# High and low parts of x computed once, kept in DRAM, and loaded by five later stages

## The chip, the cores and the metric

The kernel runs on one core of one Trainium2 chip. The core has a matrix engine (TensorE, PE in the profile; its weight loads are PEld), a vector engine (DVE), a scalar engine (ACT), a general engine (POOL) and a sequencer that here issues all DMAs (SP). Each engine works through its own instructions in order and waits on semaphores for the others. Tiles lie in the on-chip memory (SBUF), matmul results in PSUM; DRAM is reached by DMA, and all DMAs of this kernel go through one queue, fed by SP, onto 16 DMA engines. The metric is device time in microseconds (us). Three runs of the kernel before took 1255.81, 1256.64 and 1258.46 us; the median is 1256.64 us.

## The reference, cut to what matters

One decoder layer over 2048 tokens of width 1024. What is computed:

```python
hdn = rmsnorm(x, norm_gain[i])
proj = jnp.einsum("bsd,de->bse", hdn, w_in[i])
q_a, k_a, v_a, g_a, q_b, k_b, v_b, g_b = jnp.split(proj, split_at, axis=-1)
# mixer A: 8 query heads, 2 key heads, causal window of 128 tokens, attention sinks
q_a = rope(rmsnorm(q_a...), pos); k_a = rope(rmsnorm(k_a...), pos)
o_a, _, _ = banded_attention(q_a, k_a, v_a, A_WINDOW - 1, sinks=sinks_a[i])
o_a = o_a * jax.nn.silu(g_a)
# mixer B: 8 heads, patterns (128,1), (512,4), (2048,16), merged by their denominators
q_b = rope(rmsnorm(q_b...), pos); k_b = rope(rmsnorm(k_b...), pos)
o_b = dilated_attention(q_b, k_b, v_b) * jax.nn.silu(g_b)
mixed = jnp.concatenate([o_a, o_b], axis=-1)
x = x + jnp.einsum("bse,ed->bsd", mixed, w_out[i])
```

All of it is float32. The part that matters here is the product `hdn @ w_in`: its left factor x is the same for all of its columns.

## The kernel before

**Stages.** The work is cut into eight stages (`STAGES`): B0 to B3 (two heads of mixer B each), A0 and A1 (four heads of mixer A each), and O0 and O1 (half of the output projection's columns each). A stage walks over the 2048 tokens in eight halves of 256 tokens (`hf` 0 to 7; two of them make one block `sb`). For each half it makes the q/k/v projection of two groups of 128 tokens (matmuls 384 wide, or 256 wide in O), then the gate projection (256 wide), and hands the result to attention work that is issued in between.

**Three matmuls for one product.** TensorE takes float32 in the rounded form `float32r`. To keep the precision, each factor is split into a high part (the value rounded to float32r) and a low part (the rest), and `mm3` (L241 to L244) adds three products, high*high, high*low and low*high. So a half of x (1 MB, eight chunks of 128 rows by 256 tokens) needs its high parts `xh` and low parts `xl` on the chip.

**Where x comes from.** `x_load` (L145 to L149) loads half of a half, 512 KB, from the input `xT` (or from `mx`, the gated attention output, in O) into a tile `xs`, of which there are two. `x_split` (L151 to L158) takes a quarter: ACT copies it into `xh`, rounding it (L155), and POOL or DVE subtracts (L157): POOL for the quarters 0 and 1, and for all quarters of the halves 6 and 7, DVE for the rest. Six pairs of `xh` and `xl` take turns (`XB`), four for the current half and two of the next. Each of the eight stages does this for each half anew; only the very first half goes another way (`first_half`, in eight pieces). The quarters 2 and 3 of the next half are split during the gate matmuls of the current one, because their tiles are those that these matmuls read last.

**What else a half does.** In B0, `squares` sums x*x for the norm, `rstd` makes the inverse root, `rb_make` spreads it over the partitions, and `rope_tables` makes the rotary tables. POOL's `klz` (L90) writes zeros once, at the start. In each half `norm_rope` takes the projection from PSUM, `norm_factors` (POOL, L182 and L437, `fac`) and `norm_split` (DVE, L447) normalise it, and `finish` transposes q and k on TensorE. A B stage stores q, k, v, gates and sums to DRAM (`qd`, `kd`, `ld`, `vd`, `gd`, `od`), and the next stage loads them by residue class (`units_D`: `cq`, `ck`, `cl`, `cv`); at the end of such a unit the softmax factors go to DRAM (`rD`) and come back spread over the partitions (`Rb`, one buffer, two rounds of two loads), and POOL multiplies with them (L899 to L906).

**Weights.** During the last half of a stage and the first of the next, the next stage's weights come in twelve tiles (eight `stg` of the projection, L118, and the gates', L131; three buffers) and are split by ACT and DVE (`split_w`).

**What sets the order.** The program is written in Python as one stream in which attention units are interleaved with projection chunks by estimated costs (`advance`, `pcost`). A scheduler then sets each engine's order of instructions by a timeline of its own; so DMAs from different places of the program stand mixed on SP's queue, and a changed instruction can move others.

Of the kernel before, what the change touches and what calls it, by code (L numbers as in the profile page):

```python
# [18 lines left out]
KC = DM // 128  # L19
EPS = 1e-6  # L20
WB = 9
XB = 6
QB = {"Q": 2, "qc": 2}
SB = 3
BIG = 1e30
# [3 lines left out]
def f32(ap):  # L29
    return ap.bitcast(F32)  # L30
# [3 lines left out]
def hybrid_layer(ctx, tc, xT, xn, x, wB, wA, wO, ng, gains, sinks, rot, masks, ident, out):  # L34
# [9 lines left out]
    def dram(shape, name, dt=F32):  # L44
        return tc.dram_tile(shape, dt, name=name)
# [44 lines left out]
                nc.gpsimd.tensor_scalar(zt, mk[z, 0:640], 0.0, None, op0=OP.mult)  # L90

    rs_row = [dram([256], f"rsr{hf}") for hf in range(8)]
    mx = [dram([128, KC, 256], f"mx{hf}") for hf in range(8)]

    def bcast_row(d, lo, n, parts=128):
# [44 lines left out]
    XG = {}  # L140

    XS = {}
    SQ = []

    def x_load(si, hf, g):  # L145
        src = mx[hf] if STAGES[si][0] == "O" else xT[hf]
        f = xp.tile([128, 4, 256], F32, name="xs")
        nc.sync.dma_start(f, src[:, 4 * g:4 * g + 4, :])
        XS[si, hf, g] = f  # L149

    def x_split(si, hf, g):  # L151
        f = XS[si, hf, g // 2][:, 2 * (g % 2):2 * (g % 2) + 2]
        h = xp.tile([128, 2, 256], F32R, name="xh", bufs=XB)
        l = xp.tile([128, 2, 256], F32R, name="xl", bufs=XB)
        nc.scalar.activation(h, f, AF.Copy)  # L155
        eng = nc.gpsimd if g < 2 or hf >= 6 else nc.vector
        eng.tensor_tensor(l, f, f32(h), op=OP.subtract)  # L157
        XG[si, hf, g] = (h, l)  # L158

    def first_half():  # L160
        for g in range(4):
            if g % 2 == 0:
                XS[0, 0, g // 2] = xp.tile([128, 4, 256], F32, name="xs")
            f = XS[0, 0, g // 2][:, 2 * (g % 2):2 * (g % 2) + 2]
            h = xp.tile([128, 2, 256], F32R, name="xh", bufs=XB)
            l = xp.tile([128, 2, 256], F32R, name="xl", bufs=XB)
            for c in range(2):
                nc.sync.dma_start(f[:, c], xT[0][:, 2 * g + c, :])
                W[0][2](2 * g + c, lambda: (nc.scalar.activation(h[:, c], f[:, c], AF.Copy),
                                            nc.vector.tensor_tensor(l[:, c], f[:, c], f32(h[:, c]), op=OP.subtract)))  # L170
            XG[0, 0, g] = (h, l)
        for g in range(2):
            squares(XS[0, 0, g], g)

# [71 lines left out]
    def proj(si, sb):  # L246
# [22 lines left out]
        for half in range(2):  # L269
            hf = 2 * sb + half  # L270
            nx = next_half(si, hf)
            xg = [XG.pop((si, hf, g)) for g in range(4)]
            TC, TS = TB.pop((si, hf))
            if nx:
                x_load(*nx, 0)
            t1s = []
            un = wk.tile([128, 2, nh], F32, name="un")
            for tt in range(2):
                i = 2 * half + tt
                T = 4 * sb + i  # L280
                pj = ps.tile([128, 384], F32, name="sc" if early and half else "pj", bufs=2)
                for c in range(KC):
                    xh, xl = xg[c // 2]
                    s = slice(tt * 128, tt * 128 + 128)
                    mm3(pj, (xh[:, c % 2, s], xl[:, c % 2, s]), wq[c], c, c == 0, c == KC - 1)
                    if last and half == 1 and tt == 1:
                        W[si + 1][2](c)
                    if nx and tt == 1 and c == 3:
                        x_split(*nx, 1)
                    yield 490  # L290
                if tt == 0 and nx:
                    x_load(*nx, 1)
# [18 lines left out]
                nc.vector.scalar_tensor_tensor(vt[:, :, 1, :], vs, rst[:, T:T + 1], f32(vt[:, :, 0, :]),  # L311
                                               op0=OP.mult, op1=OP.subtract)
# [203 lines left out]
    def proj_out(si, sb, wq, wg, last):  # L516
# [4 lines left out]
        for half in range(2):  # L521
            hf = 2 * sb + half
            nx = next_half(si, hf)
            xg = [XG.pop((si, hf, g)) for g in range(4)]
            if nx:
                x_load(*nx, 0)
                x_load(*nx, 1)
# [512 lines left out]
```

## Time and profile before

The profiled execution took 1261.51 us; its span, from the first instruction to the last, is 1259.4 us, and what lies around it 2.1 us.

| what | busy, us | share of the span |
|---|---|---|
| TensorE matmuls | 1174.8 | 93% |
| DVE | 850.7 | 68% |
| ACT | 834.7 | 66% |
| POOL | 680.4 | 54% |
| DMA queue of the kernel, mean of 16 engines | | 59.3% |

The matmul time is that of the records, which overlap and whose ends are modelled: two matmuls in flight count once, so 93% is not 93% of the engine's peak. The granted TensorE clock was 0.969 of full speed on average. In the DMA part, 196752 packets moved 219.37 MB on the kernel's queue.

The stages can be found by the loads of x: B0 ends at about 157 us, B1 at 330, B2 at 504, B3 at 677, A0 at 850, A1 at 1006, and O0 at 1172. A stage's attention work runs partly in the next stage.

### The profile page before, as it was taken

Reading aid. Unit: us, or ns where it says so; the run is one execution under the profiler, and the core shown is the slowest. Engines: PE = TensorE matmul, PEld = TensorE weight load, DVE = VectorE, ACT = ScalarE, POOL = GpSimd, SP = SyncE. Lnnn points to the kernel's source line nnn. Section 1 sums busy time; section 2 is a strip of 40 time slices with the busy share of each in tenths; the row PEclk is TensorE's granted clock in tenths of the full one; section 3 lists DMA queues with packets and bytes.
Section 4 is the critical chain, followed back from the end, with each engine's and each line's share of the span. In section 5 each row is a group of like instructions: output and inputs, shape, how many; then the busy total and the mean of one; then the engine's idle time right before and its main releaser. Section 6 shows DMA issues by size and latency. Waiting matters only on the chain.

```text
span 1259.4 us, 25438 instructions
## 1 busy us (share of the span) xinstructions
PE 1174.8 (93%) x8328; PEld 1141.3 (91%) x8328; DVE 850.7 (68%) x2288; ACT 834.7 (66%) x2418; POOL 680.4 (54%) x788
## 2 busy tenths in 40 slices
PE   6898979899899798899998999999999999999899
PEld 5898979899799798888997999898899998999898
DVE  5676768678677678776777788789868877522221
ACT  6477868678677687676777677677776776522221
POOL 4886734566645574536576567565655554333122
PEclk9899989999899899899998999999999999999999
DMA  7454677877687667687775764545333225566561
GB/s 215 120 166 127 193 226 212 229 200 212 182 250 207 210 190 201 189 244 204 199 210 172 228 203 143 150 137 167 114 97 94 80 89 165 163 192 211 166 191 69
DMA packets 196883, 220.98 MB, mean 175 GB/s; under 512 B 34312, under 2 KB 143632, under 8 KB 196752
## 3 DMA queue, kind: packets, MB, share of 16 engines
q1 hardware_dynamic: 196752, 219.37, 59.3%
q8 instruction: 66, 1.08, 0.4%
q14 instruction: 65, 0.53, 0.1%
HBM read 164.44 MB, written 54.86 MB: 174 GB/s over the span
## 4 chain that ended last, share of the span: by engine, by line
PE 55%; DMA 16%; DVE 10%; ACT 8%; POOL 6%; issue 3%; SPq 2%; POOLq 0%; ACTq 0%; DVEq 0%
PE pj L244 39%; DMA xs<-in_xT 3%; DMA Rb<-rD 2%; DMA stg<-in_wB 2%; PE po L849 2%; DMA stg<-in_wO 2%; DMA stg<-in_wA 2%; PE sc L590 1%; PE sc L591 1%; PE po L645 1%; PE pt L828 1%; PE po L735 1%; PE pt L719 1%; ACT P L599 1%; DVE ptl L574 1%
## 5 line engine op out<-in xcount | busy, mean ns | idle before, releaser
L244 PE MATMUL pj<-wh,xh 128*128 128x384 f32 (+1 forms) x1008 | 332.8, 332 | 12.2 <-ACT wh L104 5.5
L244 PE MATMUL pj<-wl,xh 128*128 128x384 f32 (+1 forms) x1008 | 334.4, 332 | 0.8 <-DVE wl L102 0.7
L244 PE MATMUL pj<-wh,xl 128*128 128x384 f32 (+1 forms) x1008 | 333.4, 331 | 1.3 <-DVE xl L157 1.3
L157 POOL TENSOR_TENSOR xl<-xs,xh 128x512 fp32r<-128x512 f32 x158 | 210.3, 1341 | 146.3 <-ACT xh L155 136.6
L155 ACT ACTIVATE xh<-xs 128x512 fp32r<-128x512 f32 x252 | 154.5, 629 | 123.6 <-PE pj L244 100.6
L244 PEld LDWEIGHTS pj<-wh,xh 128*128 128x128 f32 x1008 | 194.0, 193 | 15.7 <-ACT wh L104 5.8
L244 PEld LDWEIGHTS pj<-wl,xh 128*128 128x128 f32 x1008 | 194.8, 193 | 3.2 <-DVE wl L102 1.1
L244 PEld LDWEIGHTS pj<-wh,xl 128*128 128x128 f32 x1008 | 194.4, 193 | 3.0 <-DVE xl L157 1.6
L574 DVE TENSOR_TENSOR ptl<-pt,pth 128x512 fp32r<-128x512 f32 (+3 forms) x232 | 142.0, 619 | 35.5 <-ACT pth L573 31.8
L244 PE MATMUL pj<-xh,wgh 128*128 128x256 f32 x496 | 147.7, 298 | 17.9 <-DVE V L311 12.0
L244 PE MATMUL pj<-xh,wgl 128*128 128x256 f32 x496 | 145.8, 294 | 0.0
L244 PE MATMUL pj<-xl,wgh 128*128 128x256 f32 x496 | 145.4, 293 | 0.0
L573 ACT ACTIVATE pth<-pt 128x512 fp32r<-128x512 f32 (+3 forms) x232 | 123.1, 543 | 23.1 <-PE pt L719 8.1
L431 POOL TENSOR_TENSOR t<-t,t 128x256 f32<-128x256 f32 (+1 forms) x96 | 78.1, 814 | 77.9 <-DVE t L422 57.2
L244 PEld LDWEIGHTS pj<-xh,wgh 128*128 128x128 f32 x496 | 97.8, 197 | 19.7 <-ACT klz L502 5.9
L244 PEld LDWEIGHTS pj<-xl,wgh 128*128 128x128 f32 x496 | 97.8, 197 | 0.6
L244 PEld LDWEIGHTS pj<-xh,wgl 128*128 128x128 f32 x496 | 97.4, 196 | 0.9 <-DVE wgl L105 0.2
L814 ACT ACTIVATE P<-P,scD 128x256 f32<-128x256 f32 (+3 forms) x128 | 71.6, 560 | 33.6 <-DVE scD L813 32.9
L157 DVE TENSOR_TENSOR xl<-xs,xh 128x512 fp32r<-128x512 f32 x94 | 76.9, 823 | 21.1 <-ACT xh L155 20.5
L447 DVE TENSOR_TENSOR t<-t,fac 128x256 f32<-128x256 f32 (+1 forms) x96 | 67.4, 710 | 30.8 <-POOL fac L182 23.7
L182 POOL TENSOR_TENSOR fac<-un,mhalf 128x8 f32<-128x8 f32 (+1 forms) x48 | 85.4, 1779 | 2.5
L813 DVE CUSTOM_DVE_ANT_0 P<-sc,mk 128x256 f32<-128x256 f32 (+3 forms) x128 | 61.1, 484 | 32.2 <-PE sc L809 31.5
(188 smaller groups left out, 3082.8 us busy)
## 6 DMA issues: line engine op xcount, KB each, us to landing
xs<-in_xT SPq DMA_DIRECT2D x94, 512.0 KB
xs<-mx SPq DMA_DIRECT2D x32, 512.0 KB
vd<-V SPq DMA_DIRECT2D x64, 128.0 KB
qd<-qc SPq DMA_DIRECT2D x32, 256.0 KB
TT<-tab SPq DMA_DIRECT2D x32, 256.0 KB
cv<-vd SPq DMA_DIRECT2D x32, 256.0 KB
cq<-qd SPq DMA_DIRECT2D x32, 256.0 KB
ck<-kd SPq DMA_DIRECT2D x64, 128.0 KB
```

Source lines behind the costliest of these rows:

```text
L155: nc.scalar.activation(h, f, AF.Copy)
L157: eng.tensor_tensor(l, f, f32(h), op=OP.subtract)
L182: nc.gpsimd.tensor_tensor(y, u, mhalf.to_broadcast([128, n]), op=OP.pow)
L244: nc.tensor.matmul(o, a, b, start=first and n == 0, stop=last and n == 2, skip_group_check=True)
L431: nc.gpsimd.tensor_tensor(t1[:, :n], t1[:, :n], t2[:, :n], op=OP.add)
L447: nc.vector.tensor_tensor(t1v, t1v, fac[:, tt, :, None].to_broadcast([128, nh, 64]), op=OP.mult)
L573: nc.scalar.activation(hi, pt, AF.Copy)
L574: nc.vector.tensor_tensor(lo, pt, f32(hi), op=OP.subtract)
L590: nc.tensor.matmul(sc[:, j, :], q[h // 2][:, h % 2, i, :], kw, start=True, stop=False)
L813: nc.vector.tensor_tensor_reduce(pd, o[:, :m], m2[:, 512 - m:], -0.125, BIG, OP.add, OP.min, nb)
L814: nc.scalar.activation(pd, pd, AF.Exp, bias=nb, scale=-1.0, accum_out=l)
L849: nc.tensor.matmul(po[:, o:o + w], a, b, start=n_ == 0, stop=n_ == len(seq) - 1, skip_group_check=True)
```

## The change

In the first stage, high and low part of a quarter now lie in one tile, and at the start of each half the four tiles are also stored to a DRAM buffer `xd` (eight buffers of 2 MB, 16.8 MB in all). In the stages B1 to A1 (`kept`), `x_load` loads these tiles as they are, four loads of 512 KB per half in place of two, all issued at the start of the half before, and `x_split` does nothing. The O stages work as before. There is one pool of eight tiles of 4 KB per partition, `x`, for loaded x and for pairs, where there were two `xs` and six pairs; the space is the same, 32 KB per partition. In the profile of the changed kernel all these tiles are called `x`.

```diff
-XB = 6
+XB = 8
...
+    xd = [dram([128, 4, 1024], f"xd{hf}") for hf in range(8)]
...
+    def x_parts():
+        t = xp.tile([128, 2, 2, 256], F32R, name="x", bufs=XB)
+        return t, t[:, 0], t[:, 1]
+
+    def kept(si):
+        return 0 < si and STAGES[si][0] != "O"
+
     def x_load(si, hf, g):
+        if kept(si):
+            for k in (2 * g, 2 * g + 1):
+                t, h, l = x_parts()
+                nc.sync.dma_start(f32(t).rearrange("p a c n -> p (a c n)"), xd[hf][:, k])
+                XG[si, hf, k] = (t, h, l)
+            return
         src = mx[hf] if STAGES[si][0] == "O" else xT[hf]
-        f = xp.tile([128, 4, 256], F32, name="xs")
+        f = xp.tile([128, 4, 256], F32, name="x", bufs=XB)
         nc.sync.dma_start(f, src[:, 4 * g:4 * g + 4, :])
         XS[si, hf, g] = f
 
     def x_split(si, hf, g):
+        if kept(si):
+            return
         f = XS[si, hf, g // 2][:, 2 * (g % 2):2 * (g % 2) + 2]
-        h = xp.tile([128, 2, 256], F32R, name="xh", bufs=XB)
-        l = xp.tile([128, 2, 256], F32R, name="xl", bufs=XB)
+        t, h, l = x_parts()
         nc.scalar.activation(h, f, AF.Copy)
         eng = nc.gpsimd if g < 2 or hf >= 6 else nc.vector
         eng.tensor_tensor(l, f, f32(h), op=OP.subtract)
-        XG[si, hf, g] = (h, l)
+        XG[si, hf, g] = (t, h, l)
+
+    def x_use(si, hf):
+        ts = [XG.pop((si, hf, g)) for g in range(4)]
+        if si == 0:
+            for g in range(4):
+                nc.sync.dma_start(xd[hf][:, g], f32(ts[g][0]).rearrange("p a c n -> p (a c n)"))
+        return [t[1:] for t in ts]
...
-            xg = [XG.pop((si, hf, g)) for g in range(4)]
+            xg = x_use(si, hf)
             TC, TS = TB.pop((si, hf))
             if nx:
                 x_load(*nx, 0)
+                if kept(nx[0]):
+                    x_load(*nx, 1)
...
                 if tt == 0 and nx:
-                    x_load(*nx, 1)
+                    if not kept(nx[0]):
+                        x_load(*nx, 1)
                     x_split(*nx, 0)
```

`first_half` and `proj_out` change in the same way (one tile for both parts; `x_use` in place of the pop). The scheduler makes a new order of it. Three places follow; a row is an instruction (line, operation, what it writes and reads, shape, and how often in a row), and the changed kernel's line numbers are about 24 higher.

The first is SP's queue just after the first half's pieces have been issued, in B0 (`xs`, then `x`: loads of the second half; `stg`: gate weights; `xd_101`: the first half's kept parts). Before:

```order
L131 DMA stg<-in_wB 128x2x128 x3
L148 DMA xs<-in_xT 128x1024
L78 DMA idf<-in_ident 128x128
L80 DMA mk<-in_masks 128x768
L148 DMA xs<-in_xT 128x1024
L399 DMA tab_0_220<-TT 128x512
L131 DMA stg<-in_wB 128x2x128
```

And now:

```order
L132 DMA stg<-in_wB 128x2x128 x3
L179 DMA xd_101<-x 128x1024 x4
L423 DMA tab_0_224<-TT 128x512
L132 DMA stg<-in_wB 128x2x128
L162 DMA x<-in_xT 128x1024 x2
L78 DMA idf<-in_ident 128x128
L80 DMA mk<-in_masks 128x768
```

The four stores of the first half stand ahead of the second half's loads, of the last gate weights and of the masks.

The second is POOL at the same time (`TT`: rotary tables; `pth`, `ptl`, `klz`: zeros written once; `rst`: inverse root; `fac`, `t`, `hl`: normalising q and k). Before:

```order
L396 TENSOR_TENSOR TT<-TT,gt 128x2x64 x4
L84 TENSOR_SCALAR pth<-idf 128x128
L85 TENSOR_SCALAR pth<-idf 128x128
L84 TENSOR_SCALAR ptl<-idf 128x128
L85 TENSOR_SCALAR ptl<-idf 128x128
L157 TENSOR_TENSOR xl<-xs,xh 128x512
L90 TENSOR_SCALAR klz_89<-mk 64x640 x2
L90 TENSOR_SCALAR klz_90<-mk 64x640 x2
L182 TENSOR_TENSOR rst<-rss,mhalf 128x2
```

And now:

```order
L420 TENSOR_TENSOR TT<-TT,gt 128x2x64 x4
L203 TENSOR_TENSOR rst<-rss,mhalf 128x2
L461 TENSOR_TENSOR un<-un,eps_84 128x8
L203 TENSOR_TENSOR fac<-un,mhalf 128x8
L455 TENSOR_TENSOR t_344<-t_344,t_345 128x256
L455 TENSOR_TENSOR t_400<-t_400,t_401 128x256
L482 TENSOR_TENSOR hl<-t_344,hl 128x128
L483 TENSOR_TENSOR hl<-t_344,hl 128x128
L482 TENSOR_TENSOR hl<-t_400,hl 128x128
L483 TENSOR_TENSOR hl<-t_400,hl 128x128
L172 TENSOR_TENSOR x<-x 128x512
```

The first half's inverse root and normalising now come before the zeros and before the second half's first split.

The third is SP's queue at the end of B1, where B2's weights come in (`Rb`: the spread softmax factors; `xd_102`: B2's second half). Before:

```order
L881 DMA rD_3_4420<-rr 16x128
L131 DMA stg<-in_wB 128x2x128
L391 DMA TT<-tab_1_317 128x512
L219 DMA RB<-rsr_94 128x256
L890 DMA Rb<-rD_3_4420 64x512
L148 DMA xs<-in_xT 128x1024
L890 DMA Rb<-rD_3_4420 64x512
L131 DMA stg<-in_wB 128x2x128
```

And now:

```order
L905 DMA rD_3_4338<-rr 16x128
L119 DMA stg<-in_wB 128x384
L157 DMA x<-xd_102 128x1024
L339 DMA vd_2193<-V 4x32x256
L132 DMA stg<-in_wB 128x2x128
L157 DMA x<-xd_102 128x1024 x2
L132 DMA stg<-in_wB 128x2x128
L157 DMA x<-xd_102 128x1024
L415 DMA TT<-tab_1_324 128x512
L914 DMA Rb<-rD_3_4338 64x512
L132 DMA stg<-in_wB 128x2x128
```

Four loads of x stand between the store of the factors and the first load of `Rb`, and among the gate weights, where one stood between the two loads of `Rb`.

More of the change, by code (lines that the diff above doesn't have):

```diff
@@ L157, in x_split @@
         eng.tensor_tensor(l, f, f32(h), op=OP.subtract)
-        XG[si, hf, g] = (h, l)
+        XG[si, hf, g] = (t, h, l)
[5 more added lines that the diff above has]
+        return [t[1:] for t in ts]
     def first_half():
+        for g in range(2):
+            XS[0, 0, g] = xp.tile([128, 4, 256], F32, name="x", bufs=XB)
         for g in range(4):
-            if g % 2 == 0:
-                XS[0, 0, g // 2] = xp.tile([128, 4, 256], F32, name="xs")
             f = XS[0, 0, g // 2][:, 2 * (g % 2):2 * (g % 2) + 2]
-            h = xp.tile([128, 2, 256], F32R, name="xh", bufs=XB)
-            l = xp.tile([128, 2, 256], F32R, name="xl", bufs=XB)
+            t, h, l = x_parts()
             for c in range(2):
@@ L170, in first_half @@
                                             nc.vector.tensor_tensor(l[:, c], f[:, c], f32(h[:, c]), op=OP.subtract)))
-            XG[0, 0, g] = (h, l)
+            XG[0, 0, g] = (t, h, l)
         for g in range(2):
@@ L523, in proj_out @@
             nx = next_half(si, hf)
-            xg = [XG.pop((si, hf, g)) for g in range(4)]
+            xg = x_use(si, hf)
             if nx:
```

## The prediction, made before the run

> **What bounds the kernel now.** I first read the stages: busy time of each engine in B0 to B3, A0, A1, O0 and O1, and at the right the granted clock, the DMA engines' share and GB/s.
>
> ```profile
> core 0: us, PE busy (x) PEld busy (x) DVE busy (x) ACT busy (x) POOL busy (x), PEclk, DMA share, GB/s
> 0.00:157.00 157.00, 136.66 (x890) 132.97 (x891) 107.77 (x252) 110.00 (x297) 110.81 (x152) 0.96 0.57 164
> 157.00:330.00 173.00, 158.68 (x1089) 154.34 (x1088) 126.39 (x352) 128.89 (x379) 90.62 (x113) 0.96 0.76 213
> 330.00:504.00 174.00, 159.25 (x1070) 154.19 (x1069) 125.33 (x336) 128.74 (x373) 99.66 (x118) 0.94 0.72 208
> 504.00:677.00 173.00, 158.06 (x1070) 152.95 (x1070) 124.44 (x342) 127.38 (x369) 98.02 (x123) 0.95 0.73 207
> 677.00:850.00 173.00, 167.79 (x1188) 162.47 (x1189) 136.59 (x410) 127.22 (x397) 109.56 (x123) 0.98 0.58 171
> 850.00:1006.00 156.00, 151.27 (x1090) 145.41 (x1089) 127.99 (x365) 116.79 (x367) 86.90 (x90) 1.00 0.35 109
> 1006.00:1172.00 166.00, 159.70 (x1261) 156.31 (x1259) 85.10 (x210) 80.75 (x218) 65.39 (x58) 0.99 0.53 166
> 1172.00:1260.00 88.00, 83.36 (x678) 82.70 (x678) 17.10 (x26) 14.95 (x24) 19.42 (x15) 0.97 0.42 138
> ```
>
> TensorE has most of every stage, but in B1 to B3 it is idle for 14 to 15 us of 173 by the records, and its clock falls to 0.94 to 0.96. There the DMA engines are busy for three quarters of the time, as busy as ACT and DVE: the stages that lose the splits are also those with the fullest DMA queue. A1 is the opposite, with a DMA share of 0.35.
>
> Then the waits, to see who holds up whom.
>
> ```profile
> POOL xl L157 <- ACT xh L155: 136.6, 41, 10.7
> ACT xh L155 <- PE pj L244: 100.6, 58, 8.5
> ...
> POOL o1c L899 <- DMA Rb<-rD: 58.3, 15, 8.2
> ```
> ```profile
> PE pj L244 <- DVE V L311: 13.2, 7, 5.7
> PE sc L244 <- POOL xl L157: 1.6, 1, 1.6
> PE pj L244 <- DVE xl L157: 1.3, 1, 1.3
> ```
>
> The split looks expensive: ACT stands still for 100.6 us until the gate matmuls release a tile, and POOL for 136.6 us behind ACT. But TensorE waits for a low part only twice, 2.9 us in all, against 13.2 us for DVE's `V`. The splits are made in time; they can cost only through what stands behind them on their engines.
>
> So I followed the chain of waits (start, length, what) from B1 to A1 (157 to 1006 us). Of it I give the two loads of x, the first, longest and last of its 30 pieces of split (14.3 us in all), and the first and the last of the 24 other DMA pieces that it has in B1 to B3 and of the 11 in A0 and A1.
>
> ```profile
> 157.64 5.71 DMA stg<-in_wB
> ...
> 170.87 0.53 ACT xh L155
> ...
> 533.54 5.27 DMA xs<-in_xT
> ...
> 593.02 4.39 DMA xs<-in_xT
> ...
> 669.66 5.22 DMA stg<-in_wA
> ...
> 684.88 2.24 DMA stg<-in_wA
> ...
> 867.57 2.30 DVE xl L157 x2
> ...
> 882.28 2.03 DMA stg<-in_wO
> ...
> 892.92 0.52 ACT xh L155
> ```
>
> x is 9.7 + 14.3 = 24 us of the chain in the five stages that change. The 24 other DMA pieces in B1 to B3, weights (`stg`), softmax factors (`rD`, `Rb`) and the spilled q, k and v, make about 98 us, four times as much.
>
> **The change, part by part.**
>
> *Removed:* per stage 32 copies on ACT and 32 subtractions, 20 on POOL and 12 on DVE (halves 6 and 7 wholly on POOL).
>
> ```profile
> L155 ACT ACTIVATE xh<-xs 128x512 fp32r<-128x512 f32 x252 | 154.5, 629 | 123.6 <-PE pj L244 100.6
> L157 POOL TENSOR_TENSOR xl<-xs,xh 128x512 fp32r<-128x512 f32 x158 | 210.3, 1341 | 146.3 <-ACT xh L155 136.6
> L157 DVE TENSOR_TENSOR xl<-xs,xh 128x512 fp32r<-128x512 f32 x94 | 76.9, 823 | 21.1 <-ACT xh L155 20.5
> ```
>
> In five stages that is 160 x 0.629 = 101 us of ACT, 100 x 1.341 = 134 us of POOL and 60 x 0.823 = 49 us of DVE, beside TensorE's work. On the path it is worth at most the chain's 24 us: 18 in B1 to B3, 6 in A0 and A1. Where such a piece goes, the next one (a weight tile, `Rb`) is late a little after, so I count two thirds in B (-12 us) and in A (-4 us); bounds 0 and -24.
>
> *Added:* 80 loads and 32 stores of 512 KB (0.524 MB): 58.7 MB on 219. One costs the DMA engines 0.524 MB at the rate when all are busy: 213 / 0.76 = 280 GB/s in B1, 138 / 0.42 = 329 GB/s in O1, so 1.6 to 1.9 us. Sixteen more loads a stage are 26 to 30 us of 173: the share in B1 to B3 goes from about 0.74 to 0.90, in A0 to 0.74, in A1 to 0.53. SP issues them in 16 x 0.34 to 0.49 us (its rows below), 5 to 8 us a stage; I count it at nothing, because SP loses its long waits for the old `xs` tiles, and at 8 us a stage if that cover is gone.
>
> ```profile
> SPq L148 <- POOL xl L157: 48.9, 30, 8.3
> ```
>
> What a DMA loses behind a load of x shows in the two rounds of `Rb`: start and length from the chain, the load ahead of it from SP's instructions.
>
> ```profile
> 238.20 3.00 DMA Rb<-rD
> ...
> 420.18 4.38 DMA Rb<-rD
> ...
> 563.70 5.65 DMA Rb<-rD
> ```
> ```profile
> 416.44 0.49 SPq L148 DMA_DIRECT2D xs<-in_xT  x1
> ...
> 560.88 0.33 SPq L148 DMA_DIRECT2D xs<-in_xT  x1
> ```
>
> 3.0 us with none ahead, 4.4 and 5.7 with one issued 3 to 4 us before. Now four come together, 6.4 to 7.5 us of queue in a half of 21.7 us (a third of the time), in place of two single ones. A DMA issued at any moment waits 1/3 x 3.5 = 1.15 us behind them, against 3.5/21.7 x 0.9 = 0.15 before: 1.0 us more. On 24 pieces that is +24 us if each counts; many are not near a burst or have another chain beside them, so I take half, +12 us in B (0 to +24). In A0 and A1 the 11 pieces meet a queue with more gaps: +4 us (0 to +11). The third place of the order above is the worst case: `Rb` and the gate weights of B2 stand behind four loads, each of which first waits until the last half's gate matmuls free its tile. Behind `Rb` POOL stands still (58.3 us already), then `fac`, DVE's `t`, and TensorE's transposes.
>
> The Trainium skill (DMA: Bandwidth & Descriptors, Specifications) gives about 358 GB/s as a core's HBM limit. By it B1's 213 + 16 x 0.524 MB / 173 us = 262 GB/s would leave over a quarter free, and the queue terms would be near 0. The rows say 280 to 329 GB/s for this mix of packets, and I go by them.
>
> *B0, the stores.* 32 x 1.6 to 1.9 = 51 to 60 us of DMA in a stage whose share is 0.57: it becomes 0.9. At the start the order is worst.
>
> ```profile
> 13.09 0.34 SPq L148 DMA_DIRECT2D xs<-in_xT  x1
> ...
> 16.07 0.33 SPq L148 DMA_DIRECT2D xs<-in_xT  x1
> ```
> ```profile
> 14.61 0.42 DVE L170 TENSOR_TENSOR xl<-xs,xh 128x256 fp32r<-128x256 f32 x1
> ```
> ```profile
> 20.20 0.34 PE L244 MATMUL sc<-wh,xh 128*128 128x384 f32 x1
> ...
> 31.58 0.69 PE L211 MATMUL po<-idf,rst 128*128 128x128 f32 x2 [4.29 <-POOL rst L182]
> ```
>
> The stores wait for the last split, at 15.0 us, and take 6.4 to 7.5 us of queue; only then come the second half's loads, that went out at 13.1 and 16.1. So its first matmul (20.2) is about 7 us later. Part of that is filled: the first half's normalising now stands ahead on POOL, and the 4.3 us before 31.58 were lost anyway. I take +5 us (0 to +9). The other 28 stores (45 to 53 us) fit the gaps of 137 us; x waits behind them now and then: +1 us (0 to +8).
>
> *At nothing:* the new load's wait for DRAM data, since the store is over 100 us older; without that cover, one load's 4 to 5 us. The common pool: in B1 to A1 a tile is free when the half two back has ended, a half before it is needed. O0 and O1: same work. The clock: it falls where TensorE pauses, and I count as many pauses as before; 0.01 more or less of it in B1 to B3 is 5 us, which the range takes in.
>
> *Sum:* -12 + 12 in B1 to B3, -4 + 4 in A0 and A1, +6 in B0: +6 us. The profiled execution, span 1259.4 and 2.1 us around it, becomes 1267.5 us; it lay 4.9 us above the median, so against runs like the three shown I say **1262.6 us**, 0.5% slower.
>
> **The rivals.**
>
> *Faster, relief wins.* ACT and POOL no longer stand still in order (100.6 and 136.6 us), so all that queues behind a split comes earlier, and the bursts are prefetches that nobody needs at once. For it: ACT and DVE are at 0.73 in B, and two loads of x on the chain go. Against it: the two short waits of TensorE. If all 24 us go, the queue costs half of its 16 us and B0 its 6: 1256.6 - 24 + 8 + 6 = 1247 us; without queue cost 1239 us. It decides where all 24 go and the queue costs under 15 us. The limit that the Trainium skill's page gives, above, speaks for this case.
>
> *Much slower, DMA becomes the bound in B1 to B3.* At a share of 0.90 each wait for weights, `Rb` and q/k/v feels the queue: the full +24 and +11, B0's upper +17, and relief of only 16: 1256.6 + 36 = 1293 us, half of that 1275. It decides from where SP comes to the bursts before the tiles are free and holds the queue. Against it: x bursts are early by a half, and the rings run empty between.
>
> *No change.* The new loads hide, the removed work was hidden, B0's stores are filled by other work: 1256 to 1259 us.
>
> *The change doing something else than it says* I exclude: 160 copies and subtractions leave the order of ACT, POOL and DVE, and 112 DMAs come into SP's.
>
> **How the numbers follow.** What a measurement of this kernel tells from no change is about 0.2%, 2.5 us. Slightly slower (1259.5 to 1272) 0.36; much slower (above) 0.13; within 0.2% 0.15; faster 0.36. So slower 0.49, same 0.15, faster 0.36. The range leaves a tenth on either side: 1240 to 1284 us. The forecast's own range is 1259.5 to 1272.
>
> **What would show it.** Right: DMA share about 0.9 in B1 to B3 and B0; ACT there at 0.62 and POOL under 0.45; more time on `Rb`, `stg` and `cq` in the chain; the second half's first matmul past 25 us; B0 5 us or more longer. Wrong, to the fast side: B1 to B3 shorter than 168 us each with the same `Rb` lengths, or B0 still ending at 157 us. Wrong, to the slow side: B1 to B3 over 180 us, or TensorE waiting for `x` loads themselves.

## The result and the profile after

The changed kernel takes 1292.2 us (median of four runs, 1289.4 to 1297.4) against 1256.2 us (1255.6 to 1258.5) before on the same chip: a ratio of 1.029, 95% interval 1.025 to 1.033, so 36 us slower. The forecast was 1262.6 us in a range of 1240 to 1284: the sign is right, the size is not, and the range does not hold it. The profiled execution spans 1288.8 us.

The stages of the changed kernel, each from its own boundaries: length, busy time of PE, PEld, DVE, ACT and POOL, then the granted clock, the DMA share and GB/s (B0 to B3, A0, A1, O0, O1).

```profile
0.00:152.00 152.00, 131.04 (x856) 125.88 (x857) 101.32 (x241) 102.99 (x279) 105.10 (x146) 0.96 0.84 273
152.00:329.00 177.00, 157.40 (x1059) 152.12 (x1058) 103.25 (x327) 110.06 (x338) 59.36 (x90) 0.94 0.84 247
329.00:507.00 178.00, 159.45 (x1076) 154.25 (x1074) 106.73 (x330) 113.10 (x341) 65.94 (x97) 0.95 0.84 251
507.00:687.00 180.00, 160.29 (x1075) 154.61 (x1075) 109.34 (x329) 111.34 (x340) 68.58 (x99) 0.95 0.82 246
687.00:895.00 208.00, 195.94 (x1364) 189.76 (x1363) 149.61 (x465) 135.66 (x424) 96.53 (x124) 0.96 0.71 213
895.00:1073.00 178.00, 173.75 (x1255) 168.89 (x1254) 127.41 (x396) 116.96 (x385) 78.79 (x88) 0.99 0.44 139
1073.00:1183.00 110.00, 108.71 (x888) 107.61 (x886) 48.20 (x107) 45.38 (x117) 37.28 (x31) 0.98 0.58 186
1183.00:1289.00 106.00, 96.51 (x771) 94.81 (x770) 22.44 (x39) 20.37 (x38) 23.00 (x18) 0.97 0.46 151
```

B0 to B3 of the kernel before, cut at its own boundaries in the same way:

```profile
0.00:151.00 151.00, 130.66 (x855) 127.01 (x856) 103.11 (x244) 104.28 (x282) 106.75 (x147) 0.95 0.56 161
151.00:314.00 163.00, 153.32 (x1055) 149.58 (x1054) 120.07 (x338) 124.21 (x364) 87.38 (x110) 0.97 0.77 217
314.00:487.00 173.00, 158.46 (x1065) 153.62 (x1064) 123.52 (x339) 127.20 (x369) 98.86 (x118) 0.94 0.72 207
487.00:661.00 174.00, 159.32 (x1079) 153.66 (x1078) 125.88 (x342) 128.63 (x377) 96.83 (x120) 0.95 0.74 209
```

ACT and POOL are relieved as planned: POOL falls from 87 to 99 us to 59 to 69 us in each of B1 to B3. Still these stages last 177 to 180 us, where it was 163 to 174, and their DMA share rises from between 0.72 and 0.77 to between 0.82 and 0.84. (The windows shown ahead of the prediction were cut elsewhere; their rows must not be subtracted from these.) Counted for both kernels from the first projection matmul of a stage to that of the next, O1 to its last projection matmul (worked out from the trace, us):

```
          B0     B1     B2     B3     A0     A1     O0     O1
before  145.4  163.5  173.0  173.7  205.0  179.3  110.9   99.8
after   146.8  176.8  178.2  180.1  207.4  178.3  110.2  102.1
```

B1 to B3 lose 13.3 + 5.2 + 6.4 = 25 us of the 29 us that the two profiled executions differ by. B0, where the stores are, loses 1.4, and A0 and A1 together 1.4. Only one execution of each kernel is profiled, and on one chip whole executions of the kernel before took 1249.8 to 1265.5 us, so the split among B1 to B3 isn't firm. That the loss lies in them is borne out by the run that keeps x in B1 to B3 only, below. TensorE's own work is the same: its busy time, weighed with the granted clock, is 1144 us in both (from the trace). Its idle time grew by 21 us, from 84.6 to 105.7, and the time that it lost to the lower clock by 9 us, from 31 to 39.

Who waits now? First the waits of the changed kernel, then the same waits before, then the last two in the run with half the bytes of x, an experiment described below (waiting line, what it waited for, us in total, times, longest).

```profile
PE sc L832 <- DMA ck<-kd: 14.1, 4, 5.4
POOL osum L928 <- DMA Rb<-rD: 45.1, 12, 9.6
DVE t L471 <- POOL fac L203: 63.6, 18, 11.7
```
```profile
PE sc L808 <- DMA ck<-kd: 1.6, 1, 1.6
POOL osum L904 <- DMA Rb<-rD: 16.8, 7, 4.9
DVE t L447 <- POOL fac L182: 23.7, 9, 5.7
```
```profile
POOL osum L928 <- DMA Rb<-rD: 40.6, 12, 6.5
DVE t L471 <- POOL fac L203: 51.9, 16, 8.4
```

TensorE never waits for a load of x. It waits for the spilled keys `ck`, which it hardly did before, and with half the bytes it doesn't wait for them at all. POOL waits longer for `Rb`, and DVE for the `fac` that stands behind `Rb` on POOL. But these two waits are nearly as long with half the bytes, in a kernel that is faster than the one before, so by themselves they don't show what the bytes cost. TensorE's idle time that ends with a DMA is 18 us here and 6 us with half the bytes; what ends with DVE, 44 and 21 us (sums from the trace). One place in B2 where a DMA beside the loads of x is late: SP's instructions (start, length, what, count), then TensorE's.

```profile
373.33 2.28 SPq L157 DMA_DIRECT2D x<-xd  x3
375.67 0.43 SPq L806 DMA_DIRECT2D cq<-qd  x1
376.15 0.72 SPq L809 DMA_DIRECT2D ck<-kd  x1
376.97 0.63 SPq L157 DMA_DIRECT2D x<-xd  x1
377.64 0.50 SPq L809 DMA_DIRECT2D ck<-kd  x1
```
```profile
382.11 0.34 PE L265 MATMUL pj<-wh,x 128*128 128x384 f32 x1
385.94 0.88 PE L832 MATMUL sc<-ck,cq 128*128 128x256 f32 x2 [3.49 <-DMA ck<-kd]
```

The second `ck` is issued at 377.64 behind four loads of x that went out in the 4.3 us before; TensorE can go on at 385.94, 8.3 us later, after a pause of 3.5 us. Over the whole of B1 to B3 the time from issue to the last landing (a landing is the report of one DMA engine that its part has arrived) shows the same (means in us, worked out from the landings in the trace, DMAs issued between 150 and 690 us; the third column is the experiment with half the bytes, below):

```
            before  after  half the bytes
Rb<-rD       3.64   4.39   3.92
rD<-rr       3.66   4.83   2.95
stg<-in_wB   3.90   4.74   3.92
ck<-kd       4.85   5.24   4.06
cq<-qd       4.87   5.56   4.32
cv<-vd       4.60   5.29   4.55
TT<-tab      4.44   6.65   4.89
RB<-rsr      4.65   6.91   4.74
```

The DMAs of these rows take 0.4 to 2.3 us longer than before, about 1 us as a mean; the stores `vd`, `qd`, `kd` and `gd`, not in the table, 0.1 to 0.6 us.

### The profile page after: what moved, and what is told of

It reads as the page before. It is cut to its first block, busy times and chain, and to the rows that moved or that the text cites. A ratio compares the mean times of both kernels' runs of the same rounds, so it can differ in the third digit from the quotient of the medians.

```text
span 1288.8 us, 25223 instructions
## 1 busy us (share of the span) xinstructions
PE 1183.1 (92%) x8328; PEld 1147.9 (89%) x8328; DVE 768.3 (60%) x2228; ACT 755.9 (59%) x2258; POOL 534.6 (41%) x688
## 4 chain that ended last, share of the span: by engine, by line
PE 38%; DMA 12%; DVE 5%; ACT 3%; POOL 3%; issue 2%; SPq 1%; POOLq 0%; ACTq 0%; DVEq 0%
PE pj L265 28%; DMA stg<-in_wA 3%; DMA Rb<-rD 2%; PE po L759 2%; PE pt L743 2%; DMA stg<-in_wO 1%; DMA rD<-rr 1%; PE sc L614 1%; DMA stg<-in_wB 1%; PE sc L615 1%; PE po L873 1%; POOL fac L203 1%; DVE P L622 1%; DVE ptl L598 1%; PE sc L832 1%
## 5 line engine op out<-in xcount | busy, mean ns | idle before, releaser
L265 PE MATMUL pj<-wh,x 128*128 128x384 f32 (+1 forms) x2016 | 562.1, 334 | 14.5 <-ACT wh L105 7.1
L265 PEld LDWEIGHTS pj<-wh,x 128*128 128x128 f32 x2016 | 378.5, 194 | 19.3 <-ACT wh L105 7.5
L265 PE MATMUL pj<-wl,x 128*128 128x384 f32 (+1 forms) x1008 | 335.8, 333 | 0.0
L265 PE MATMUL pj<-x,wgh 128*128 128x256 f32 x992 | 208.5, 298 | 12.0 <-DVE eA L689 6.0
L265 PEld LDWEIGHTS pj<-wl,x 128*128 128x128 f32 x1008 | 196.0, 194 | 1.8 <-DVE wl L106 0.2
L265 PEld LDWEIGHTS pj<-x,wgh 128*128 128x128 f32 x992 | 166.5, 200 | 14.4 <-ACT P L623 6.2
L265 PE MATMUL pj<-x,wgl 128*128 128x256 f32 x496 | 146.9, 296 | 0.4 <-DVE wgl L106 0.3
L265 PE MATMUL pj<-wgh,x 128*128 128x256 f32 x496 | 131.7, 288 | 3.5 <-ACT wgh L102 3.5
L265 PEld LDWEIGHTS pj<-x,wgl 128*128 128x128 f32 x496 | 98.6, 199 | 1.4 <-DVE wgl L106 0.8
L265 PEld LDWEIGHTS pj<-wgh,x 128*128 128x128 f32 x496 | 96.1, 195 | 4.2 <-ACT wgh L102 4.1
```

The costliest lines, as they stand in the source:

```text
L265: nc.tensor.matmul(o, a, b, start=first and n == 0, stop=last and n == 2, skip_group_check=True)
```

## The experiments

Three theories were to be told apart. **Bytes:** the doubled bytes of x slow all other transfers in proportion. **Burst:** what costs is that four loads come together and others stand behind them on one queue. **Pool and stores:** the common pool of eight tiles or B0's stores take the time. Every ratio is to runs of the kernel before on the same chip; diffs are against the changed kernel. In all of them "kept" means loaded from DRAM as high and low parts.

### Stores and common pool, but still split in each stage

```diff
     def kept(si):
-        return 0 < si and STAGES[si][0] != "O"
+        return False
```

> The first stage stores the parts of x and the tiles share one pool of eight, as in the changed kernel, but no stage loads what was stored: every stage splits x itself. Theory (the bytes of x in B1 to B3 delay the weights, Rb and the spilled q and k): the time stays near the kernel before, 1256 to 1262 us, B0 about 1 to 3 us longer. Rival (the scheduler's new order and the common pool cost the time, whatever is loaded): half of the loss or more is here, 1272 us or above.

Measured: 1277.7 us, ratio 1.015 (1.008 to 1.021). Stores and pool together cost about 18 us, with an uncertainty of 8. The theory that only the loads' bytes cost misses.

### The same traffic without the loads

```diff
     def kept(si):
-        return 0 < si and STAGES[si][0] != "O"
+        return False
...
-        if si == 0:
-            for g in range(4):
+        if STAGES[si][0] != "O":
+            for g in range(4 if si == 0 else 2):
```

> Every stage splits x itself, and in B1 to A1 two of the four pairs of each half are stored to DRAM again, where nobody reads them: 1 MB more per half in these stages, as many bytes as the changed kernel adds there, without any relief of ACT, POOL and DVE. Theory of bytes: as slow as the changed kernel or slower, 1285 to 1315 us, with the loss in B1 to B3. Rival of order: near the run with the stores in B0 alone. Rival of position (what counts is that four loads stand together and ahead of others on SP's queue): under 1275 us, since stores stand elsewhere and wait for nothing.

Measured: 1300.1 us, 1.032 (1.024 to 1.039). Against the run before, 41.9 MB more, as stores, cost another 1.7% (0.7 to 2.7), and by the profiles the loss is in B1 to B3: 536 for 512 us. Traffic costs time here even if hardly an instruction waits for it: all waits that end with a landing of these stores come to 2.3 us.

### Half the bytes

```diff
-                nc.sync.dma_start(f32(t).rearrange("p a c n -> p (a c n)"), xd[hf][:, k])
-                XG[si, hf, k] = (t, h, l)
+                nc.sync.dma_start(f32(h).rearrange("p c n -> p (c n)"), xd[hf][:, k, 0:512])
+                XG[si, hf, k] = (t, h, h)
```

> As the changed kernel, but the five stages load only the high part (256 KB in place of 512 KB, four loads per half as there) and use it in place of the low part too, so the bytes per stage are those of the kernel before and the splits are gone. Theory of bytes: the relief shows alone, 1235 to 1258 us, DMA share in B1 to B3 back near 0.75. Rival of order, and rival of SP waiting for tiles: the same instructions stand at the same places, so 1280 us or more.

Measured: 1252.0 us, 0.994 (0.991 to 0.997): faster than before, with the loads at the same places, as many of them, and as many matmuls. This kernel leaves out the low parts of x in B1 to A1, so its output is another one. What differs in its work from the changed kernel is 256 KB for 512 KB per load. The stages B1 to B3 of this run, and its queue in all beside that of the changed kernel (packets, MB, share of the DMA engines):

```profile
150.00:317.00 167.00, 155.65 (x1068) 152.04 (x1067) 106.35 (x330) 112.45 (x341) 59.24 (x89) 0.96 0.75 214
317.00:486.00 169.00, 156.86 (x1068) 151.73 (x1068) 106.45 (x329) 111.63 (x341) 68.47 (x98) 0.97 0.74 213
486.00:655.00 169.00, 157.70 (x1069) 152.59 (x1068) 105.97 (x328) 110.54 (x339) 68.90 (x101) 0.97 0.75 213
```
```profile
q1 hardware_dynamic: 212880, 236.15, 62.8%
```
```profile
q1 hardware_dynamic: 212880, 278.10, 70.3%
```

The number of packets is the same in both; only their size differs. The loads of x then move as much per half as the kernel before (1 MB), and the DMA share is back at its 0.74 to 0.75: at equal bytes the change would gain 0.6%. The doubling of x costs 1.029 - 0.994 = 3.5%, 43 us (37 to 50 by the two intervals). By the two profiles, which differ by 44 us, B1 to B3 take 31 us of it, A0 11 us and A1 nothing (-1 us).

### Kept in A0 and A1 only

```diff
-        return 0 < si and STAGES[si][0] != "O"
+        return STAGES[si][0] == "A"
```

> Only A0 and A1 load the kept parts; B1 to B3 split x as before. Theory of bytes: A0 and A1 have room in the DMA queue (shares 0.58 and 0.32 before), so no loss beyond a few us: 1252 to 1264 us. Rival of order: any of these orders may lose, no statement on the sign, but not the same stages; rival of position: A0 and A1 lose 5 us each, 1265 us or more.

Measured: 1275.0 us, 1.015 (1.008 to 1.023), the same as with nothing kept (1.015), within 1%. In A0 and A1 relief and queue cancel as far as that tells. The time is outside the 1252 to 1264 us, which left out what stores and pool cost.

### Two loads and two, in place of four together

```diff
             if nx:
                 x_load(*nx, 0)
-                if kept(nx[0]):
-                    x_load(*nx, 1)
...
                 if tt == 0 and nx:
-                    if not kept(nx[0]):
-                        x_load(*nx, 1)
+                    x_load(*nx, 1)
```

> The changed kernel with its four loads per half issued two and two: the first two at the start of the half, the others after the first group's projection, where the second load stood before. Same bytes. Theory of bytes (the DMA engines are full, whoever stands first): 1284 to 1298 us. Rival of the burst (four together delay what stands behind them): 1262 to 1280 us.

Measured: 1282.7 us, 1.017 (1.012 to 1.022), between the two expectations. Spreading the burst wins 1.2% (0.5 to 1.9), 15 us: a third of the 43. Yet the landings in B1 to B3 are no shorter than in the changed kernel (means from the trace: `Rb` 4.2 for 4.4 us, `stg` 5.0 for 4.7, `ck` 5.3 for 5.2). So the mean time from issue to landing doesn't set the cost alone.

### The loads of x on a queue of their own

```diff
-                nc.sync.dma_start(f32(t).rearrange("p a c n -> p (a c n)"), xd[hf][:, k])
+                nc.scalar.dma_start(f32(t).rearrange("p a c n -> p (a c n)"), xd[hf][:, k])
```

> The changed kernel with the loads of the kept parts issued by ACT, so on a DMA queue of their own, while all else stays on SP's queue. Same bytes, and ACT issues 160 DMAs (about 64 us of it at 0.4 us each, less than the 101 us of copies that it lost). Theory that the loss is waiting in line (weights, Rb and spilled tiles stand behind x in one queue, and SP waits for x's tiles): 1255 to 1278 us. Rival that the loss is bandwidth (the queues share the 16 engines): 1284 us or more.

Measured: 1289.9 us, 1.023 (1.020 to 1.026). A separate queue wins 0.6%, and the intervals overlap. The run doesn't decide between the two, though the time is the rival's. TensorE's waits for `ck` do fall, from 14.1 us to 0.6. But ACT now issues the loads and waits for their tiles itself, and TensorE's idle time that ends with ACT rises from 32 to 58 us (sums from the trace). And both queues take the same eight semaphores (last section), so the two lines aren't independent.

### The common pool alone

Nothing stored, nothing kept; only the pool of eight tiles remains of the change.

```diff
...
-        return 0 < si and STAGES[si][0] != "O"
+        return False
...
-        if si == 0:
+        if si < 0:
```

> The common pool of eight tiles alone: nothing is stored or kept, every stage loads x and splits it as before. The run with the stores alone lost 1.45% (about 18 us) although nothing read the stores, mostly in B1 and A0. Theory (the pool, with the order that the scheduler makes of it, costs these 18 us): 1268 to 1282 us. Rival (B0's stores cost them): 1254 to 1262 us.

Measured: 1272.0 us, 1.010 (1.007 to 1.014). ACT's wait for the raw x, in this run and then before:

```profile
ACT x L170 <- DMA x<-in_xT: 98.5, 46, 6.6
```
```profile
ACT xh L155 <- DMA xs<-in_xT: 12.8, 5, 5.3
```

Raw halves and split pairs now take tiles from one ring, so a load waits until the matmuls have released a pair, and comes late to the split: 98.5 us of waiting in place of 12.8. That this wait is what the 1% goes to is likely but not shown. It needs splits from raw x in B1 to A1; where x is kept there, only B0, O0 and O1 still split.

### The stores alone, with the pools of before

```diff
-XB = 8
+XB = 6
...
-        return 0 < si and STAGES[si][0] != "O"
+        return False
...
-        f = xp.tile([128, 4, 256], F32, name="x", bufs=XB)
+        f = xp.tile([128, 4, 256], F32, name="xs")
...
```

> The stores of B0 with the pools of the kernel before (two tiles of loaded x, six pairs); nothing is kept. Theory (the pool costs the 18 us): 1255 to 1264 us. Rival (the stores): 1270 us or more. If this and the run of the pool alone both lose, the scheduler's order is sensitive to any such edit.

Measured: 1266.5 us, 1.006 (1.004 to 1.009), between the two expectations: the run with 16.8 MB of stores is 8 us slower. So this run and that of the pool alone both lose, and the third case of the expectation isn't ruled out: part of both losses can be the order that the scheduler makes of any such edit. In the profile B0, where the stores are, is no longer than before (144.5 for 145.4 us); B1 and A1 are 9 and 8 us longer, A0 8 us shorter.

### A quarter of the bytes, in one load for a half

```diff
-            for k in (2 * g, 2 * g + 1):
+            if g == 0:
                 t, h, l = x_parts()
-                nc.sync.dma_start(f32(t).rearrange("p a c n -> p (a c n)"), xd[hf][:, k])
-                XG[si, hf, k] = (t, h, l)
+                nc.sync.dma_start(f32(t).rearrange("p a c n -> p (a c n)"), xd[hf][:, 0])
+                for k in range(4):
+                    XG[si, hf, k] = (t, h, l)
```

> As the changed kernel, but the five stages load one quarter per half, 512 KB, and use it for all four: a quarter of the changed kernel's bytes there and half of the kernel before's. (With half the bytes, in four smaller loads, the ratio was 0.994.) Theory (each byte in the queue costs, before the change too): clearly faster than with half the bytes, 1225 to 1245 us. Rival (below a DMA share of about three quarters nothing waits for the queue any more, only the splits' relief counts): 1245 to 1256 us.

Measured: 1224.6 us, 0.974 (0.968 to 0.980). Fewer bytes go on paying below the level of before. (This kernel uses one quarter of each half of x in place of all four in B1 to A1, so its output is another one.) This alone doesn't say whether it is the bytes or the three loads that are gone; the last run tells.

### Kept in B1 to B3 only

```diff
-        return 0 < si and STAGES[si][0] != "O"
+        return 0 < si and STAGES[si][0] == "B"
```

> Only B1 to B3 load the kept parts; A0 and A1 split x as before. Theory (the loss of bytes lies in the stages with the full queue; loading in A alone changed nothing against the stores alone): the ratio of the changed kernel, 1.02 to 1.035. Rival (the loss comes from all five alike): 1.015 to 1.02.

Measured: 1308.0 us, 1.040 (1.035 to 1.045), slower than both expectations and than with all five stages kept. A0 and A1 again split raw x out of the common pool here; their lengths are 211 and 183 us against 207 and 178 in the changed kernel, which is part of the difference. Against the run with stores and common pool, which splits in every stage, B1 to B3 are 27 us longer (539 for 512 us) and A0 and A1 together 3 us shorter (lengths from the traces). So the loss of the changed kernel is in B1 to B3.

### Kept in all five, with pools of their own and two and two

The pools are as before, six pairs and two `xs`; the last quarter of a kept half lies in an `xs` tile, and the loads come two and two.

```diff
-XB = 8
+XB = 6
...
-                t, h, l = x_parts()
-                nc.sync.dma_start(f32(t).rearrange("p a c n -> p (a c n)"), xd[hf][:, k])
+                if k < 3:
+                    t, h, l = x_parts()
+                    flat = f32(t).rearrange("p a c n -> p (a c n)")
+                else:
+                    t = xp.tile([128, 4, 256], F32R, name="xs")
+                    h, l = t[:, 0:2], t[:, 2:4]
+                    flat = f32(t).rearrange("p a n -> p (a n)")
+                nc.sync.dma_start(flat, xd[hf][:, k])
...
```

The lines left out put raw x into `xs` tiles again and issue the loads two and two as above.

> The changed kernel with the pools of the kernel before (six pairs, two tiles of loaded x; of the four kept tiles of a half three are pairs and one is a tile of the other pool) and its loads two and two. Theory (the common pool costs 1% and the burst 1.2%, both go): ratio 1.004 to 1.014, 1263 to 1276 us. Rival (the gain of two and two already holds the pool's share, or the order decides): 1.015 to 1.025.

Measured: 1280.0 us, 1.017 (1.012 to 1.022), the same as two and two with the common pool (1.017). The expected gain from the pools isn't there: where all five stages keep x, the common pool costs nothing that can be measured (0.0%, uncertain by 0.7%). The 1% of the pool belongs to kernels that split in B1 to A1.

### The same, kept in A0 and A1 only

```diff
-        return 0 < si and STAGES[si][0] != "O"
+        return STAGES[si][0] == "A"
```

(with the other lines of the run before)

> The same pools, two and two, and only A0 and A1 load the kept parts, where the DMA queue has room. Theory: the stores cost 0.6%, relief and bytes in A are about equal: ratio 0.997 to 1.008. It is the one of these that could beat the kernel before; relief of the whole 6 us in A without a cost would give 1.000. Rival (A's relief is worth more once the pool is out of the way): below 0.997.

Measured: 1265.1 us, 1.005 (1.002 to 1.008), against 1.006 for the stores alone. The best version that computes everything and stores x is still slower than before; keeping x in A0 and A1 brings 0.1%, nothing that can be told. No kernel of the study that does the whole computation beats the one before.

### A quarter of the bytes, in four loads at the old places

What was open: whether the gain of the single load came from bytes or from the number of loads.

```diff
-                nc.sync.dma_start(f32(t).rearrange("p a c n -> p (a c n)"), xd[hf][:, k])
-                XG[si, hf, k] = (t, h, l)
+                nc.sync.dma_start(f32(h[:, 0]), xd[hf][:, k, 0:256])
+                h = h[:, 0:1].to_broadcast([128, 2, 256])
+                XG[si, hf, k] = (t, h, h)
```

> As the changed kernel, with four loads per half at the same places, but each of 128 KB in place of 512 KB (one chunk's high part, used for both chunks and for the low part): a quarter of the bytes, the same number of loads and tiles. Theory (bytes alone): as the run with one load of 512 KB, ratio 0.970 to 0.980. Rival (tiles and count made that run's further gain, and below half the bytes nothing more is won): as the run with half the bytes, 0.989 to 0.998. Between the two, both count.

Measured: 1221.9 us, 0.974 (0.969 to 0.980), the same as with one load. So at these bytes the number of loads doesn't matter; the bytes do. (This kernel leaves out half of the high parts and all low parts in B1 to A1.) Its stages B1 to B3:

```profile
150.00:308.00 158.00, 152.84 (x1071) 149.03 (x1070) 106.19 (x329) 112.26 (x340) 59.15 (x89) 0.99 0.71 200
308.00:473.00 165.00, 154.62 (x1057) 149.70 (x1056) 105.51 (x329) 111.64 (x339) 68.50 (x98) 0.97 0.68 192
473.00:633.00 160.00, 154.57 (x1080) 150.22 (x1079) 107.55 (x328) 111.66 (x341) 68.91 (x101) 0.99 0.70 197
```

DVE, ACT and POOL work as long as in the run with half the bytes, and nearly as long as in the changed kernel; only the DMA share, the granted clock and the time move. The three runs that load x in four pieces at the same places make a line (ratio times 1256 us):

```
MB of x in B1 to A1   ratio    us against the row above   us per MB
       21.0           0.9741
       41.9           0.9942          +25                    1.2
       83.9           1.0288          +43                    1.0
```

By the intervals the two steps are 0.8 to 1.6 and 0.9 to 1.2 us per MB. In the profiles of the three, TensorE's work at full clock is 1141, 1142 and 1144 us, its idle time 58, 72 and 106 us, and the time lost to the lower clock 21, 30 and 39 us (from the traces). So more bytes make pauses, and the lower clock adds 9 us in each step. Whether the other numbers that the first two compute with change the clock was not tested.

## Why the prediction was wrong in size

The kernels between before and after give a sum that can be laid beside the prediction's, each step a difference of two measured ratios, times 1256 us:

```
                                    predicted     measured   from
stores                                 +6            +8      stores alone with old pools: 1.006
relief (B and A)                      -16           -15      from there to half the bytes: 0.994
doubled bytes of x (B and A)          +16           +43      from there to the change: 1.029
common pool                             0             0      two and two, common against own pools
sum                                    +6           +36
```

The measured steps add up by construction, since each begins where the last one ended.

**The relief** was sized right: -15 us (10 to 20 by the intervals) where -16 was said. That path goes from own pools to the common one. From the run with stores and common pool it is -25 us, but part of that is the late raw loads, which vanish with the splits.

**The queue term** is the step that failed: "I take half, +12 us in B (0 to +24)", with +4 in A. It measured 43 us, more than both upper ends together (35). Its price per DMA was near, 1.0 us more: the landings above say about 1 us. It had been read from three pieces, though, and one more `Rb` of the same chain, at 488.49, took 4.50 us with weights (`stg`) and no load of x shortly ahead. What fell short is the count. It was taken from the 24 pieces of one chain of one execution, and then halved, as if a late transfer could only cost where it already stood on that chain. But the transfers in the rows above were all slower, and some that had been in time came onto the path: TensorE's waits for `ck` went from one to four. In B3, the only B stage whose chain the changed kernel's profile gives whole, the chain's DMA pieces other than x went from 9 (37.5 us) to 13 (70.2 us). So there was reason to raise the count, not to halve it. That count and price together make up the 43 us is not shown: 9 us of the step are lower clock, and the run with two loads and two lost 15 us less with landings as long. In another measure: the 80 loads' 41.9 MB beyond half the bytes cost 43 us, 0.54 us for each 0.524 MB, a third of the 1.6 to 1.9 us that 0.524 MB keeps the DMA engines busy.

**The share** of 0.90 in B1 to B3 was not reached, 0.82 to 0.84. The added loads took less of the engines than 26 to 30 us a stage: 0.84 x 178 - 0.74 x 173 = 22 us, and the stages became longer.

**The stores** cost in all what was said, but not where. TensorE of the changed kernel at the start:

```profile
23.71 0.80 PE L265 MATMUL pt<-x,wgh 128*128 128x256 f32 x2 [2.65 <-ACT wgh L105]
...
26.64 0.69 PE L265 MATMUL sc<-wh,x 128*128 128x384 f32 x1
```

The second half's first matmul comes at 26.6 us (20.2 before), past the 25 us foretold, though the pause ahead of it is for gate weights (`wgh`) and not for x. Yet the third half's first matmul comes earlier (40.8 for 47.2 us, from the trace), and B0 as a whole loses 1.4 us in the profile. The run with the stores alone is 8 us slower, and B0 isn't longer there either, so the 8 us fall behind B0. Why they do, by another order of the instructions or otherwise, stays open.

**At nothing:** SP's issues were put there because SP would lose its long waits for tiles. It does wait for them less (48.9 us for `xl` alone before):

```profile
SPq L157 <- PE pj L265: 20.4, 30, 2.6
```

But it stands longer for landings (last section), so what the issues cost isn't told apart. They are as many with half the bytes, so they are not in the 43 us. The clock was put at nothing on the count of "as many pauses as before". The pauses grew, and the lower clock took 9 of the 29 us by which the two profiled executions differ; in B1 to B3 of the run with a quarter of the bytes in four loads it rose to between 0.97 and 0.99. The pool was rightly at nothing for the change, where B1 to A1 keep x; where they split raw x, it costs 1%.

**A0 and A1** were right in sum: -4 + 4 = 0 against 1.4 us in the profile and 0.1% in the run that keeps x there alone. The terms were larger in A0, if the two profiles can be trusted so far: the doubled bytes took 11 us there. In A1 the DMA share rose only to 0.44, and they took nothing.

**The rivals.** The time is that of the "much slower" case (1293 us), but not by its mechanism. It was to decide "from where SP comes to the bursts before the tiles are free and holds the queue"; that wait is 20.4 us in 30 pieces. DMA did not become the bound either: at a share of 0.84 TensorE still has 89% of these stages. Its +24 +11 in full was nearer the truth than the forecast's half, its B0 term of 17 us twice too large. The "faster" rival wanted all 24 us of relief and a queue below 15 us; 15 and 43 us came. Without the doubled bytes the kernel is faster, by 0.6%.

The Trainium skill (DMA: Bandwidth & Descriptors, Specifications) gives about 358 GB/s as a core's HBM limit. As an amount of traffic the trace doesn't contradict it: 246 to 251 GB/s in B1 to B3. The prediction's use of it, that below it the queue would cost near 0, fails in these stages: on 213 or 214 GB/s another 33 to 38 GB/s cost 31 us by the profiles, and 192 to 200 GB/s were faster still. In B0 it doesn't fail: 273 GB/s for 161 cost 1.4 us.

**The chances.** Slower had 0.49, and the case that came 0.13. The range ended at 1284, because the full price of the queue was held for a rare case that needed saturated engines. The cost came without saturation, at a share of 0.82 to 0.84.

## What to carry to other kernels

Where DMAs with results that are needed soon are in flight most of the time (here B1 to B3, at a share of 0.74), count added bytes as a cost on the path even if the new transfers themselves are early: here about a third of their time on the DMA engines, 1 us per MB over B1 to A1. It isn't a price for every stage: B0 took 16.8 MB more for 1.4 us, and A1 took its 8.4 MB for nothing. To load again what the other engines can compute paid here only without added bytes: the splits were worth 1.2%, the doubled bytes 3.5%. And in this kernel fewer bytes pay at once (21 MB less of x: 2%), so look for those before relieving engines that are not on the path.

## What the runs showed of the hardware that was not expected

**Bytes cost time below a full queue, without a threshold in the range that was measured.** Loads of x cost 1.2 and 1.0 us per MB, over B1 to A1, while the DMA share of B1 to B3 went from about 0.70 to 0.75 and from there to 0.84, although no single wait of TensorE is for x. The cost as stores was about half (41.9 MB, 1.7%, 21 us; 9 to 34 by the intervals). The share alone doesn't tell the cost: in B0 the share rose from 0.56 to 0.84 with 16.8 MB of stores, and B0 took 142.7 to 148.3 us in the 13 profiled kernels with these stores, 145.4 before (from the traces). Why B0 is spared was not tested.

**At most eight DMAs are in flight.** The DMAs take eight semaphores in turn, and in every trace all landings of one come before the next issue on the same semaphore. So the ninth waits for the first, whatever it carries. SP stands still for landings 153 us before, 226 us in the changed kernel, 128 us with half the bytes, and 301 us with the loads on ACT's queue, which takes the same eight semaphores (sums from the trace). Of the 226 us, 68 are for landings of `x<-xd`; with half the bytes it is 10.5 us, with a quarter in four loads none. The three longest of those waits in the changed kernel, all in front of DMAs of other lines (columns as above):

```profile
SPq L812 <- DMA x<-xd: 9.1, 10, 1.3
SPq L809 <- DMA x<-xd: 8.7, 8, 1.5
SPq L784 <- DMA x<-xd: 8.0, 11, 1.2
```

How much of the 43 us goes through this limit, and how much through the DMA engines' time, was not separated: no run changed the number of DMAs in flight.
